# Ending a layer in PSUM: identity products for the residual, sums and squares on ScalarE, a written order, and two changes beside it

## The chip, the cores and the metric

The kernel runs on one core of one Trainium2 chip. The metric is the device time of one execution in microseconds (us), measured without the profiler as a median of several runs; the trace comes from one more execution, taken under the profiler. Engines are named as the profile names them: PE is TensorE's matmul, PEld its weight load, DVE is VectorE, ACT is ScalarE, POOL is GpSimd, and SP is SyncE, which here only issues transfers.

## The reference, cut to what matters

A two-layer encoder over 512 tokens of width 1024. Each layer is a mixer (attention in layer 0, a gated linear recurrence in layer 1) and then a mixture of 16 experts. Each sublayer ends in a residual sum and a layer norm:

```
h = layer_norm(ALPHA * h + mixed, *norm1[layer])
h = layer_norm(ALPHA * h + grouped_moe(h, router_w, router_bias, *experts[layer]), *norm2[layer])
```

The router gives each token two experts with gates that sum to one. An expert computes `silu(t @ w1) * (t @ w3)`, then `@ w2`, and its rows are scaled by the gates and summed. `layer_norm` subtracts the mean, divides by the root of the variance plus 1e-5, and applies a gain `g` and a bias `b`.

## The kernel before, in words

All matrix work is done in fp32r pairs: a weight or an activation is split into a rounded high part H (a cast on ACT, L131 for weights) and a low part L (a subtraction on DVE, L132), and a product takes three matmuls. Weights come as 1 MB chunks in order of use over the SP queue into rings of buffers; `Stream.conv_to(n)` converts parts up to the n-th. The order of instructions on each engine is set when the program is built, by a scheduler that takes what it holds to be ready, earlier lines first. Inside `tc.manual_schedule` the named engines keep the order in which the code is written; `issue_after(x)` puts an engine's instructions behind x on that engine.

**From the router to expert 0.** `route_tail` ends the first layer norm tile by tile (four tiles of 128 tokens), stores the normalized rows to `hbuf` in HBM, and computes for each token its two experts as one-hot rows `oh`, and its places in their lists (`route_p` on PE, `route_v` on DVE). At most CAP = 96 tokens of an expert are handled at once. Two small products per tile give `idx`, the list of tokens of each expert (L478, L480). `moe` then gathers expert 0's 96 rows from `hbuf` by an indirect transfer on POOL (`gather`, L552), transposes them on PE (`x_t`, L565), splits them into H and L (L566, L567), and starts the first products (`w13`, L583 to L588).

**An expert.** `w13` is 48 matmuls of 512 columns, `glu` an activation (L594) and a multiplication (L595), `h_t` four transposes (L603) and a split (L604, L605), and `w2` 24 matmuls (L629 to L631) into two PSUM banks `py`. `scatter` scales `py` by the gate on ACT (L639, two halves) and adds the 96 rows to `ybuf` in HBM by an indirect accumulating transfer on POOL (L640). To hide `glu` and `h_t`, `jobs` sets expert e's `w13` ahead of expert e-1's `w2`; only the last expert is different: the order there is `w13(14) w2(13) w2(14) w13(15) w2(15)`.

**The end of a layer.** When all scatters have landed, four accumulating transfers on POOL add `ybuf` to the residual rows `hs[t]` in SBUF (L780; ALPHA has been multiplied in before). Expert 15 is not scattered: `direct` multiplies a one-hot matrix `ot` with its scaled rows on PE (L664, L665, two halves per tile, `pd`). `tail` then does the second layer norm by a string TAIL of steps: `a` (or `p` and `q` for the halves) adds `pd` to `hs[t]` on DVE and sums the rows (L801), `m` computes the mean and the squares (L325 on DVE, L330 on ACT), `v` or `g` subtracts the mean and multiplies the gain (L809, L834, DVE), `e` or `v` takes the root (L335 on DVE, L336 on POOL), `h` multiplies it and adds the bias (L813, DVE), `k` does the same on ACT and POOL (L818, L819), and `f` hands the tile on. In layer 0 `f` is `feat_tile`: transposes on PE (L1054) and the split of the next mixer's input (L1057 on ACT, L1058 on DVE), and the mixer's first products (L1072 to L1074) take tiles 0 and 1 first. In layer 1 `f` stores the tile to `out` (L1732). Layer 0's tail is in written order on ACT and DVE, layer 1's is not.

PSUM has eight banks: tag `h` four, tags `t` and `r` two each.

Of the kernel before, what the change touches and what calls it, by code (L numbers as in the profile page):

```python
# [19 lines left out]
P = 128  # L20
D = 1024
# [9 lines left out]
TAIL = ("p0 q0 m0 p1 q1 m1 e0 p2 g0 e1 h0 q2 m2 g1 f0 h1 p3 q3 m3 e2 f1 g2 c4 h2 e3 f2 g3 h3 f3",  # L31
        "a0 m0 a1 m1 v0 a2 m2 v1 k0 f0 a3 m3 v2 h1 f1 v3 h2 f2 h3 f3")
# [163 lines left out]
class K:  # L196
# [143 lines left out]
    def route_begin(self, l):  # L340
        self.l = l
        rp = self.rp
# [48 lines left out]
    def logits_b(self, t, q, hT):  # L391
        nc = self.nc
        pl = self.ps.tile([P, 512], F32, name=f"pl{self.l}_{t}{q}", tag="t")
        for j in range(4):
            nc.tensor.matmul(pl[:, :E], hT[:, j], self.grw[:, 4 * q + j], start=j == 0, stop=j == 3)
# [67 lines left out]
    def route_v(self, a, z):  # L463
# [7 lines left out]
        V.tensor_reduce(pos, tr, axis=AX.X, op=ALU.add)  # L471
        for t in range(a, z):
# [84 lines left out]
    def x_t(self, xg, nm):  # L557
# [3 lines left out]
        for q in range(2):  # L561
            pt = self.ps.tile([P, 4, CAP], F32, name=f"xt{nm}{q}", tag="t")
            for j in range(4):
# [44 lines left out]
    def w2(self, st, key, H, L, nm, la, last=False):  # L608
# [3 lines left out]
        for fc in range(FC):  # L612
# [19 lines left out]
            mm = []  # L632
        return py
# [10 lines left out]
    def direct(self, py, gate, src, nm):  # L644
# [64 lines left out]
    def moe(self, l, st, hs, after, on_done):  # L709
        nc, tc = self.nc, self.tc  # L710
        self.hs = hs
        self.s2 = [self.rp.tile([P, 2], F32, name=f"s2{l}{t}", tag="s1", bufs=4) for t in range(NT)]
        st.limit = st.where["moe_end", l]
        xg, X, HT, gi = {}, {}, {}, []
        seq = [e for e in range(OV + 1)] + ["o"] + [e for e in range(OV + 1, E)]

        def gather(i):
# [4 lines left out]
            gi.append(self.last_gather)  # L722
# [1034 lines left out]
```

## Time and profile before

| what | value |
|---|---|
| time, median of 3 runs (lowest, highest) | 1131.86 us (1131.6, 1134.7) |
| time of the profiled execution | 1139.46 us |
| its span, first to last instruction | 1137.5 us |
| PE busy | 1044.2 us, 92% of the span |
| DVE busy | 906.9 us, 80% |
| ACT busy | 766.1 us, 67% |
| POOL busy | 240.8 us, 21% |
| mean granted clock of TensorE | 0.957 of full speed |

The profiled execution is 7.6 us longer than the median, so stretches are read from it and differences are carried over to the median. A busy share is a mean over stages with different limits; what a change is worth is read in its own stage, from what each engine waited for there. Times in the trace are counted from the first instruction.

### The profile page before, as it was taken

To read this page: it belongs to the slowest core of one execution; us is meant where nothing else is said; L and a number is where in the kernel's file an instruction comes from. 1 tells how busy PE (TensorE), PEld (TensorE's weight loads), DVE (VectorE), ACT (ScalarE), POOL (GpSimd) and SP (SyncE) were. 2 spreads that over 40 slices of the span, in tenths; PEclk is the share of its full clock that TensorE was granted. 3 is DMA by queue.
4 is the path that set the end of the run, shared out by engine and by line. 5 is a ranking of instruction groups with operands and counts; after the bars stand their busy time and mean duration, and the time that the engine had idled before them with its cause. 6 is when DMAs were issued, how large, how long until landed. Compare 5 with 4: busy or idle time off the path is not lost. (4 is left out here: it accounts for less than half of the span.)

```text
span 1137.5 us, 14945 instructions
## 1 busy us (share of the span) xinstructions
PE 1044.2 (92%) x5010; PEld 765.1 (67%) x5010; DVE 906.9 (80%) x1481; ACT 766.1 (67%) x1112; POOL 240.8 (21%) x238
## 2 busy tenths in 40 slices
PE   7999898995999999999979999995999999998992
PEld 5677677883677777776558657774677777775651
DVE  5586778558999999997886597848999999996775
ACT  5456688333878888786744899233878888786762
POOL 1113555315123111120210000014123111120132
PEclk9898999996999999999979999996999999999996
DMA  8181010696999999989953203496999999997983
GB/s 298 56 259 38 1 38 1 229 344 208 358 327 365 361 357 359 357 306 361 311 127 120 70 14 111 155 380 206 359 316 375 362 358 365 365 335 248 332 254 101
DMA packets 132980, 281.22 MB, mean 247 GB/s; under 512 B 8905, under 2 KB 32617, under 8 KB 132769
## 3 DMA queue, kind: packets, MB, share of 16 engines
q1 hardware_dynamic: 121344, 245.20, 60.0%
q0 software_dynamic: 10928, 33.93, 12.3%
q10 hardware_dynamic: 624, 1.08, 0.3%
q8 instruction: 41, 0.67, 0.2%
q14 instruction: 43, 0.34, 0.1%
HBM read 261.41 MB, written 23.74 MB: 251 GB/s over the span
## 5 line engine op out<-in xcount | busy, mean ns | idle before, releaser
L132 DVE TENSOR_TENSOR wl<-rr,wh 128x1024 fp32r<-128x1024 f32 x180 | 212.1, 1219 | 17.3 <-ACT wh L131 16.3
L131 ACT CAST wh<-rr 128x1024 fp32r<-128x1024 f32 x180 | 180.2, 1049 | 40.2 <-PE p L587 33.0
L132 DVE TENSOR_TENSOR wl<-rf,wh 128x1024 fp32r<-128x1024 f32 x104 | 124.0, 1220 | 20.8 <-ACT wh L131 20.3
L131 ACT CAST wh<-rf 128x1024 fp32r<-128x1024 f32 x104 | 105.2, 1048 | 46.6 <-DMA rf<-l_w_out 26.0
L132 DVE TENSOR_TENSOR wl<-raw,wh 128x1024 fp32r<-128x1024 f32 (+1 forms) x101 | 119.1, 1207 | 16.9 <-ACT wh L131 16.9
L131 ACT CAST wh<-raw 128x1024 fp32r<-128x1024 f32 (+1 forms) x101 | 100.9, 1033 | 30.5 <-PE ppx L1073 8.1
L583 PE MATMUL p<-wh,xh 128*96 128x512 f32 x256 | 103.3, 404 | 1.5 <-ACT xh L566 1.5
L629 PE MATMUL py<-wh,hh 128*96 128x512 f32 x256 | 101.4, 404 | 3.0 <-ACT y L639 1.9
L630 PE MATMUL py<-wl,hh 128*96 128x512 f32 x256 | 101.5, 396 | 1.6 <-DVE wl L132 1.6
L631 PE MATMUL py<-wh,hl 128*96 128x512 f32 x256 | 101.1, 398 | 0.9 <-DVE hl L605 0.9
L585 PE MATMUL p<-wh,xh 128*96 128x512 f32 x256 | 101.2, 395 | 0.3
L587 PE MATMUL p<-wh,xl 128*96 128x512 f32 x256 | 101.4, 396 | 0.0
L584 PE MATMUL p<-wl,xh 128*96 128x512 f32 x256 | 101.3, 396 | 0.0
L586 PE MATMUL p<-wl,xh 128*96 128x512 f32 x256 | 101.0, 395 | 0.0
L588 PE MATMUL p<-wh,xl 128*96 128x512 f32 x256 | 101.0, 395 | 0.0
L640 POOL DMA_INDIRECT ybuf<-y,dst x30 | 58.9, 1964 | 178.5 <-ACT y L639 151.8
L552 POOL DMA_INDIRECT xg<-hbuf,idx x32 | 35.4, 1108 | 237.3 <-PE xt L565 199.6
L132 DVE TENSOR_TENSOR wl<-rx,wh 128x1024 fp32r<-128x1024 f32 x56 | 66.3, 1219 | 8.4 <-ACT wh L131 8.4
L131 ACT CAST wh<-rx 128x1024 fp32r<-128x1024 f32 x56 | 56.2, 1050 | 9.8 <-PE p L587 9.1
L629 PEld LDWEIGHTS py<-wh,hh 128*96 128x96 f32 x256 | 41.4, 163 | 19.8 <-ACT y L639 3.4
L631 PEld LDWEIGHTS py<-wh,hl 128*96 128x96 f32 x256 | 41.7, 163 | 19.2 <-DVE hl L605 1.8
L585 PEld LDWEIGHTS p<-wh,xh 128*96 128x96 f32 x256 | 41.5, 162 | 19.3 <-ACT wh L131 1.2
(426 smaller groups left out, 2438.9 us busy)
## 6 DMA issues: line engine op xcount, KB each, us to landing
rr<-l_w SPq DMA_DIRECT2D x124, 512.0 KB, 11.3
rf<-l_w SPq DMA_DIRECT2D x68, 512.0 KB, 13.1
rr<-l_w SPq DMA_DIRECT2D x28, 1024.0 KB, 14.2
rx<-l_w SPq DMA_DIRECT2D x36, 512.0 KB, 12.0
raw<-l_w SPq DMA_DIRECT2D x36, 512.0 KB, 13.2
rf<-l_w SPq DMA_DIRECT2D x15, 1024.0 KB, 12.6
raw<-l_w SPq DMA_DIRECT2D x13, 1024.0 KB, 8.5
raw<-l_w_in SPq DMA_DIRECT2D x11, 1024.0 KB, 5.6
```

The source lines that it names most:

```text
L131: nc.scalar.copy(h[:, :w], r[:, a:a + w])
L132: nc.vector.tensor_tensor(l[:, :w], r[:, a:a + w], h[:, :w].bitcast(F32), op=ALU.subtract)
L583: nc.tensor.matmul(p1, H[:, kc], w1h[:, sl], start=f, stop=False)
L584: nc.tensor.matmul(p1, H[:, kc], w1l[:, sl], start=False, stop=False)
L585: nc.tensor.matmul(p3, H[:, kc], w3h[:, sl], start=f, stop=False)
L586: nc.tensor.matmul(p3, H[:, kc], w3l[:, sl], start=False, stop=False)
L587: nc.tensor.matmul(p1, L[:, kc], w1h[:, sl], start=False, stop=e)
L588: self.last_mm = nc.tensor.matmul(p3, L[:, kc], w3h[:, sl], start=False, stop=e).ins
L629: nc.tensor.matmul(py[n], H[:, c], a, start=c == 0, stop=False)
L630: nc.tensor.matmul(py[n], H[:, c], b, start=False, stop=False)
L631: nc.tensor.matmul(py[n], L[:, c], a, start=False, stop=c == FC - 1)
L640: nc.gpsimd.indirect_dma_start(out=self.ybuf[l], out_offset=bass.IndirectOffsetOnAxis(ap=dst, axis=0), in_=y, in_offset=None, bounds_check ...
```

## The change

Three things are done at once.

1. **Expert 0's rows come from a product.** `route_v` makes for each tile a selection matrix `sel` (128 tokens by 96 places) from the place that each token has in expert 0's list. `first_x` multiplies the normalized tiles with it in fp32 on PE, 8 products for each tile into two banks of tag `h`; the result is expert 0's input, already transposed. The first pair of tiles is done behind the last router product, the second pair at the end of `route_tail`. `x_t` takes these banks; the gather of expert 0 and its transposes are gone, and the gathers of experts 1 and 2 are issued at once.
2. **The last experts' order.** It becomes `w13(14) w2(13) w13(15) w2(14) w2(15)`, with expert 15's `h_t` in the middle of `w2(14)`. Expert 14's scatter is then issued after `w2(14)`, which is right ahead of `w2(15)`.
3. **The tail.** `pre` multiplies the identity matrix with `hs[t]` in fp32 into the `pd` banks (two products of 512 columns per tile), and `post` accumulates expert 15's rows onto it. `s` sums the rows from PSUM on ACT (two halves), `m` computes the mean on DVE and squares the halves from PSUM on ACT, `v` subtracts the mean and multiplies the gain from PSUM on DVE into `hs[t]`, `e` adds the two sums of squares and takes the root, `h` as before. Both layers' tails are in written order on ACT and DVE. Layer 1's last tile is finished and stored in halves (`z`).

```diff
-TAIL = ("p0 q0 m0 p1 q1 m1 e0 p2 g0 e1 h0 q2 m2 g1 f0 h1 p3 q3 m3 e2 f1 g2 c4 h2 e3 f2 g3 h3 f3",
-        "a0 m0 a1 m1 v0 a2 m2 v1 k0 f0 a3 m3 v2 h1 f1 v3 h2 f2 h3 f3")
+TAIL = ("s0 m0 v0 s1 e0 m1 v1 h0 e1 s2 h1 f0 m2 v2 e2 s3 f1 h2 m3 v3 e3 f2 c4 h3 f3",
+        "s0 m0 v0 s1 e0 m1 v1 h0 f0 e1 s2 h1 f1 m2 v2 e2 s3 h2 f2 m3 v3 e3 z3")
...
         V.tensor_reduce(pos, tr, axis=AX.X, op=ALU.add)
+        p0 = wp.tile([P, n], F32, name=f"p0{l}{a}", tag=f"p0{a}", bufs=1)
+        V.tensor_tensor(p0, tr[:, 0, :, 0], tr[:, 1, :, 0], op=ALU.add)
+        for t in range(a, z):
+            self.sel[t] = wp.tile([P, CAP], F32, name=f"sel{l}{t}", tag="sel", bufs=NT)
+            V.tensor_scalar(self.sel[t], self.iota16[:, :CAP], p0[:, t - a:t - a + 1], None, op0=ALU.is_equal)
...
+    def first_x(self, u, a, z):
+        if a == 0:
+            self.x0 = [self.ps.tile([P, 512], F32, name=f"x0{self.l}{q}", tag="h", bufs=4)[:, :4 * CAP]
+                       .rearrange("p (j c) -> p j c", j=4) for q in range(2)]
+        for t in range(a, z):
+            for kc in range(KC):
+                self.nc.tensor.matmul(self.x0[kc // 4][:, kc % 4], u[t][:, kc * P:(kc + 1) * P], self.sel[t],
+                                      start=t == 0 and kc % 4 == 0, stop=t == NT - 1 and kc % 4 == 3)
...
                 nc.tensor.matmul(py[n], L[:, c], a, start=False, stop=c == FC - 1)
             mm = []
+            if fc == 1 and mid:
+                mid()
...
-        def mm(t):
+        def pre(t):
             r = []
             for n in range(2):
+                r.append(self.ps.tile([P, 512], F32, name=f"pd{nm}{t}{n}", tag="h", bufs=4))
+                nc.tensor.matmul(r[n], self.ident, self.hs[t][:, n * 512:(n + 1) * 512], start=True, stop=False)
+            return r
+
+        def post(t, r):
+            for n in range(2):
                 sl = slice(n * 512, (n + 1) * 512)
-                ps = self.ps.tile([P, 512], F32, name=f"pd{nm}{t}{n}", tag="h", bufs=4)
-                nc.tensor.matmul(ps, oh[:, t], yH[:, sl], start=True, stop=False)
-                nc.tensor.matmul(ps, oh[:, t], yL[:, sl], start=False, stop=True)
-                r.append(ps)
-            return r
-        return mm
+                nc.tensor.matmul(r[n], oh[:, t], yH[:, sl], start=False, stop=False)
+                nc.tensor.matmul(r[n], oh[:, t], yL[:, sl], start=False, stop=True)
+        return pre, post
...
-            r += [(e, "a"), (e - 1, "b")] if e < E - 1 else [(e - 1, "b"), (e, "a")]
+            r += [(e, "a"), (e - 1, "b")]
...
-        gather(0)
-        port = self.rp.tile([P, 1], F32, name=f"port{l}", tag="port")
-        with tc.issue_after(gi[0]):
-            nc.gpsimd.memset(port, 0.0)
-            gather(1)
-        X[0] = self.x_t(xg[0], f"{l}_0")
-        gather(NXG)
+
         first = st.where["moe", l]
+        gather(1)
+        gather(2)
         with tc.issue_after(self.last.ins), tc.issue_after(self.last_sig):
-            free = nc.vector.tensor_copy(self.rp.tile([P, 1], F32, name=f"free{l}", tag="port"), port).ins
-            with tc.issue_after(free):
-                st.conv_to(first + 6)
+            st.conv_to(first + 2)
+            X[0] = self.x_t(None, f"{l}_0", self.x0)
+            st.conv_to(first + 6)
...
-            py = self.w2(st, (l, e), *HT[e], nm, LA, e == E - 1)
+            def mid():
+                if e == E - 2:
+                    HT[E - 1] = self.h_t(hm, f"{l}_{E - 1}", "x")
+
+            py = self.w2(st, (l, e), *HT[e], nm, LA, e == E - 1, mid)
...
+        def s(t):
+            for n, sl in enumerate(halves):
+                nc.scalar.activation(junk[:, sl], psd[t][n], AF.Identity, accum_out=self.s2[t][:, n:n + 1])
 
         def m(t):
             st[t] = self.ln_mu(self.s2[t], f"{l}2{t}")
-            self.ln_sq(st[t], hs[t], f"{l}2{t}", "vl", self.hl2)
+            for n, sl in enumerate(halves):
+                nc.scalar.activation(junk[:, sl], psd[t][n], AF.Square, bias=st[t][0], accum_out=sq[t][:, n:n + 1])
 
         def v(t):
-            mu, ss, ve, rs = st[t]
-            V.scalar_tensor_tensor(hs[t], hs[t], mu, g, op0=ALU.add, op1=ALU.mult)
+            for n, sl in enumerate(halves):
+                V.scalar_tensor_tensor(hs[t][:, sl], psd[t][n], st[t][0], g[:, sl], op0=ALU.add, op1=ALU.mult)
+
+        def e(t):
+            V.tensor_scalar(st[t][1], sq[t][:, 0:1], sq[t][:, 1:2], None, op0=ALU.add)
             self.ln_rs(st[t])
...
+        for t in (0, 1):
+            psd[t] = pre(t)
         for t in range(NT):
-            psd[t] = mm(t)
+            if t > 1:
+                psd[t] = pre(t)
+            post(t, psd[t])
...
+        with self.tc.issue_after(self.last_pl):
+            self.first_x(u, *pairs[0])
         self.sigmoid(*pairs[1])
...
         self.route_v(*pairs[1])
+        self.first_x(u, *pairs[1])
```

## Rows read from the trace of the kernel before

**Rows 1.** Windows: stretch, length, busy PE, PEld, DVE, ACT, POOL, clock, DMA, GB/s.
```profile
300.00:545.00 245.00, 243.74 (x1190) 173.84 (x1189) 221.77 (x279) 195.82 (x243) 45.06 (x30) 1.00 1.02 350
```

**Rows 2.** Timeline of PE, layer 0, from the router to expert 0.
```profile
269.40 0.17 PE L461 MATMUL pp<-ohs,half 128*128 128x16 f16 x1 [4.85 <-DVE ohs L452]
...
277.43 1.51 PE L565 MATMUL xt<-call,xg 96*128 96x96 f32 x8 [6.02 <-DMA xg<-hbuf,idx]
278.91 0.74 PE L583 MATMUL p<-wh,xh 128*96 128x512 f32 x1
...
282.01 0.41 PE L584 MATMUL p<-wl,xh 128*96 128x512 f32 x1
```

**Rows 3.** Timeline of PE, layer 1, the same place.
```profile
781.84 0.17 PE L461 MATMUL pp<-ohs,half 128*128 128x16 f16 x1 [4.91 <-DVE ohs L452]
...
794.10 0.39 PE L584 MATMUL p<-wl,xh 128*96 128x512 f32 x1
```

**Rows 4.** Windows, layer 0, expert 0's first products.
```profile
279.00:282.00 3.00, 3.00 (x7) 1.97 (x8) 2.96 (x4) 0.46 (x1) 3.00 (x4) 0.50 0.83 312
```

**Rows 5.** Instructions on tile `ot`, durations in ns (min/median/max).
```profile
L652 DVE TENSOR_SCALAR ot<-half,row x8: 275/276/391, 553.0 to 1092.0; 96x128 fp32r<-96x128 f16 x8
```

**Rows 6.** Timeline of PE: fp32 products and transposes at either clock.
```profile
257.20 1.00 PE L395 MATMUL pl<-grw,hT 128*128 128x16 f32 x8
...
586.04 1.94 PE L1054 MATMUL ftm<-call,xr 128*128 128x128 f32 x8 [3.23 <-DVE xr L813]
...
621.58 3.60 PE L1123 MATMUL pg<-xc,gw 128*128 128x512 f32 x8
```

**Rows 7.** Timeline of PE, layer 0, the last experts.
```profile
545.38 0.39 PE L630 MATMUL py<-wl,hh 128*96 128x512 f32 x1
545.61 0.39 PE L631 MATMUL py<-wh,hl 128*96 128x512 f32 x1
546.92 0.47 PE L629 MATMUL py<-wh,hh 128*96 128x512 f32 x1 [0.93 <-ACT y L639]
...
572.06 0.39 PE L631 MATMUL py<-wh,hl 128*96 128x512 f32 x1
```

**Rows 8.** Timeline of PE, layer 1, last products of experts 13 and 15.
```profile
1082.64 0.39 PE L631 MATMUL py<-wh,hl 128*96 128x512 f32 x1
...
1110.66 0.39 PE L631 MATMUL py<-wh,hl 128*96 128x512 f32 x1
```

**Rows 9.** Timeline of ACT, layer 1, expert 13's output.
```profile
1083.22 1.26 ACT L639 ACTIVATE y<-py,gpos 96x512 f32<-96x512 f32 x2
```

**Rows 10.** Timeline of POOL, both layers: scatter of expert 14, accumulations.
```profile
556.74 2.36 POOL L640 DMA_INDIRECT ybuf<-y,dst  x1 [3.04 <-ACT wh L131]
566.14 3.62 POOL L780 DMA_DIRECT2D xr<-ybuf  x4 [7.03 <-DMA ybuf<-y,dst]
...
1093.69 2.48 POOL L640 DMA_INDIRECT ybuf<-y,dst  x1 [2.90 <-ACT wh L131]
1100.44 3.62 POOL L780 DMA_DIRECT2D xr<-ybuf  x4 [4.27 <-DMA ybuf<-y,dst]
```

**Rows 11.** Tile `xr`, 555 to 610 us: the four accumulations' transfers.
```profile
DMA to landing us min/median/max: 5.4/8.4/11.9
```

**Rows 12.** The page's transfers: issues, size, median us from issue to landing.
```profile
hbuf<-xr POOLq DMA_DIRECT2D x6, 512.0 KB, 3.3
```

**Rows 13.** Timeline, layer 0: DVE's first residual sum, the next mixer's first products.
```profile
574.45 0.69 DVE L801 SCALAR_TENSOR_TENSOR xr<-xr,pd 128x512 f32<-128x512 f32 x1 [0.50 <-PE pd L665]
...
589.20 0.80 PE L1072 MATMUL ppx<-x,wh 128*128 128x256 f32 x2 [1.22 <-ACT x L1057]
```

**Rows 14.** Timeline, layer 1: DVE's first residual sum, its last step, POOL's last root.
```profile
1111.77 0.69 DVE L801 SCALAR_TENSOR_TENSOR xr<-xr,pd 128x512 f32<-128x512 f32 x1 [0.59 <-PE pd L665]
...
1129.18 1.28 DVE L813 SCALAR_TENSOR_TENSOR xr<-xr,lw,b 128x1024 f32<-128x1024 f32 x1 [0.66 <-POOL lw L336]
...
1128.59 0.55 POOL L336 TENSOR_TENSOR lw<-lw,mhalf 128x1 f32<-128x1 f32 x1 [2.66 <-DVE lw L335]
```

More of the change, by code (lines that the diff above doesn't have):

```diff
@@ L341, in route_begin @@
         self.l = l
+        self.sel = {}
         rp = self.rp
@@ L394, in logits_b @@
         for j in range(4):
-            nc.tensor.matmul(pl[:, :E], hT[:, j], self.grw[:, 4 * q + j], start=j == 0, stop=j == 3)
+            self.last_pl = nc.tensor.matmul(pl[:, :E], hT[:, j], self.grw[:, 4 * q + j], start=j == 0, stop=j == 3).ins
         x = self.lg[:, t]
@@ L561, in x_t @@
         for q in range(2):
-            pt = self.ps.tile([P, 4, CAP], F32, name=f"xt{nm}{q}", tag="t")
-            for j in range(4):
+            pt = pts[q] if pts else self.ps.tile([P, 4, CAP], F32, name=f"xt{nm}{q}", tag="t")
+            for j in range(4 if pts is None else 0):
                 kc = 4 * q + j
@@ L606, in h_t, with w2 @@
         return H, L
-    def w2(self, st, key, H, L, nm, la, last=False):
+    def w2(self, st, key, H, L, nm, la, last=False, mid=None):
         nc = self.nc
@@ L711, in moe @@
         self.hs = hs
-        self.s2 = [self.rp.tile([P, 2], F32, name=f"s2{l}{t}", tag="s1", bufs=4) for t in range(NT)]
+        self.s2 = [self.rp.tile([P, 4], F32, name=f"s2{l}{t}", tag="s1", bufs=4) for t in range(NT)]
         st.limit = st.where["moe_end", l]
-        xg, X, HT, gi = {}, {}, {}, []
+        xg, X, HT, gi = {}, {}, {}, {}
         seq = [e for e in range(OV + 1)] + ["o"] + [e for e in range(OV + 1, E)]
@@ L783, in moe @@
         st.limit = len(st.parts)
+        conv = None
         if l == 0:
             st.conv_to(done + 2)
-            with tc.manual_schedule(engines={mybir.EngineType.Activation, mybir.EngineType.DVE}):
-                self.tail(l, py, gate, self.idx[:, E - 1:E], g, b, on_done, lambda n: st.conv_to(done + n))
-        else:
-            self.tail(l, py, gate, self.idx[:, E - 1:E], g, b, on_done)
+            conv = lambda n: st.conv_to(done + n)
+        with tc.manual_schedule(engines={mybir.EngineType.Activation, mybir.EngineType.DVE}):
+            self.tail(l, py, gate, self.idx[:, E - 1:E], g, b, on_done, conv)
     def tail(self, l, py, gate, src, g, b, on_done, conv=None):
@@ L795, in tail @@
         psd, st = {}, {}
-        mm = self.direct(py, gate, src, f"{l}_{E - 1}")
-        def a(t, ns=(0, 1)):
-            for n in ns:
-                u = hs[t][:, n * 512:(n + 1) * 512]
-                V.scalar_tensor_tensor(u, u, 1.0, psd[t][n], op0=ALU.mult, op1=ALU.add, accum_out=self.s2[t][:, n:n + 1])
+        pre, post = self.direct(py, gate, src, f"{l}_{E - 1}")
+        halves = [slice(n * 512, (n + 1) * 512) for n in range(2)]
+        full = slice(0, D)
+        junk = self.hl2.tile([P, D], BF16, name=f"tj{l}", tag="vl", bufs=HX)
@@ L815, in k, with h @@
-        def k(t):
-            for n in range(2):
-                sl = slice(n * 512, (n + 1) * 512)
-                nc.scalar.mul(hs[t][:, sl], hs[t][:, sl], st[t][3])
-                nc.gpsimd.tensor_tensor(hs[t][:, sl], hs[t][:, sl], b[:, sl], op=ALU.add)
+        def h(t, sl=full):
+            V.scalar_tensor_tensor(hs[t][:, sl], hs[t][:, sl], st[t][3], b[:, sl], op0=ALU.mult, op1=ALU.add)
         def f(t):
             on_done(t, hs[t])
-        def p(t):
-            a(t, (0,))
-        def q(t):
-            a(t, (1,))
@@ L830, in e, with z @@
-        def e(t):
-            self.ln_rs(st[t])
-        def gain(t):
-            V.scalar_tensor_tensor(hs[t], hs[t], st[t][0], g, op0=ALU.add, op1=ALU.mult)
+        def z(t):
+            for sl in halves:
+                h(t, sl)
+                on_done(t, hs[t], sl)
+        for t in (0, 1):
+            psd[t] = pre(t)
         for t in range(NT):
-            psd[t] = mm(t)
-        fn = dict(a=a, m=m, v=v, h=h, k=k, f=f, p=p, q=q, e=e, g=gain, c=conv)
+            if t > 1:
+                psd[t] = pre(t)
+            post(t, psd[t])
@@ L839, in tail @@
+        fn = dict(s=s, m=m, v=v, h=h, f=f, e=e, z=z, c=conv)
         for x in TAIL[l].split():
@@ L961, in out_proj @@
                 for t in range(NT):
-                    s1.append(self.rp.tile([P, 2], F32, name=f"s1{nm}{t}", tag="s1", bufs=4))
+                    s1.append(self.rp.tile([P, 4], F32, name=f"s1{nm}{t}", tag="s1", bufs=4))
                     for kc in range(KC - 2, KC):
@@ L1731, in build @@
         k.wp = wp = L("moe1")
-        k.moe(1, st, hs, lambda: None, lambda t, u: nc.sync.dma_start(out[0, t * P:(t + 1) * P], u))
+        k.moe(1, st, hs, lambda: None,
+              lambda t, u, sl=slice(0, D): nc.sync.dma_start(out[0, t * P:(t + 1) * P, sl], u[:, sl]))
         wp.release()
```

9 lines of the change are left out of this document (4 added, 5 removed).

## The prediction

> **What bounds the kernel now.** I read the page first, then the windows of the expert stages, then engine by engine the three places that the change touches. In the windows view PE is busy for 243.7 of 245 us between 300 and 545 us, at full clock, and DVE for 221.8 [rows 1]: the experts are bound by PE, so time that is won or lost ahead of them or behind them goes one to one into the total. Two kinds of place are left where PE waits.
>
> The first is the way from router to expert 0. The timeline of PE shows it waiting for the one-hot rows until 269.40, then for the gather until 277.43, and starting expert 0 at 278.91, at half clock [rows 2, 4]. From the one-hot rows to the eighth product of expert 0 it is 282.01 - 269.40 = 12.6 us in layer 0 and 794.10 - 781.84 = 12.3 us in layer 1 [rows 2, 3].
>
> The second is the end of a layer. DVE takes up the first residual sum at 574.45, released by PE, and the next mixer's first products start at 589.20, released by the second tile's split [rows 13]; the products run on without a gap from there. In layer 1 DVE starts at 1111.77 and begins the last step at 1129.18, for 1.28 us, so it ends at 1130.46 [rows 14]. What the reader must see beside this is the chain on POOL: expert 14's scatter goes out at 556.74, the accumulations behind it at 566.14 [rows 10], and the first of them lands no sooner than 5.4 us later [rows 11], at 571.5, or 2.9 us before DVE asks for it. This is all the slack that the chain has.
>
> **Part 1, expert 0's input by a product.** Behind the one-hot rows DVE does five short instructions (the two for the places, `p0`, two selections); none should be dearer than the 0.28 us of the nearest form [rows 5], so at most 1.4, and I take 1.2. Then come 16 fp32 products of 96 columns. The nearest rows are eight in 1.00 us at full clock and eight transposes in 1.94 us at half clock [rows 6], so 2.0 to 3.9; PE has been idle and I take 3.8, with 0.2 for the small index products among them. The first half's H copy runs under the last of them. Expert 0's eighth product starts seven steps behind its first: at full clock a step is 545.61 - 545.38 = 0.23 us [rows 7], so 1.6; before, at half clock, the seven took 282.01 - 278.91 = 3.1 [rows 2, 4]. As PE has by then run some 4 us without a pause, as it had before it regained full clock in [rows 2], I take full clock and 1.7. The first pair of tiles adds three more DVE instructions ahead of the last tile's residual, which DVE has no room for: 0.55. Its 16 products lie in the time in which PE waits for the one-hot rows (4.85 us [rows 2]); without this cover they would cost 2.0 to 3.9. For the conversions that must now come faster I set 0.3. Sum: 1.2 + 3.8 + 0.2 + 1.7 + 0.55 + 0.3 = 7.75. The gain is 12.6 - 7.75 = 4.85 and 12.3 - 7.75 = 4.5, together 9.35. Bounds: all at full clock 3.8 more; expert 0 at half clock and the conversions a part late, 2.3 less in each layer, so 4.7 to 13.1. The gathers of experts 1 and 2 are issued at once on POOL; expert 1's rows have the whole of expert 0's 48 products (11 us) to land, so they cost nothing; the last tile's store to HBM comes off the path too.
>
> **Part 2, the last experts' order.** Work on PE from the end of expert 13's `w2` is 48 + 24 + 24 products either way. Before, it waits there for the bank `py` (545.61 + 0.23 = 545.84 to 546.92, 1.1 us) and again for `glu` and the split of expert 15, and ends at 572.3 [rows 7]. After, it is 72 products (16.6) and four transposes (0.45) to the end of `w2(14)`, 1.1 for `py`, 24 products (5.5): 545.84 + 23.7 = 569.5, which is 2.8 earlier. In layer 1 the same sum gives 1082.87 + 23.7 = 1106.5 against 1110.9 [rows 8].
>
> But the scatter of expert 14 now stands at the end of `w2(14)`. In layer 0 that is 545.84 + 17.05 = 562.9. ACT's scaling of both halves ended 1.6 us after PE at the same step of expert 13 (1082.87 to 1083.22 + 1.26 [rows 8, 9]), and 0.25 goes by to the issue: 564.7, against 556.74 before, 8.0 later. In layer 1: 1099.9, 1101.8, against 1093.69, 8.1 later. From scatter to accumulations it took 9.4 us in layer 0, under the weight loads, and 6.75 in layer 1, when these were over [rows 10]; they are over at 564.7 too, so I take 6.75 for both (bounds 6.75 and 9.4). The accumulations go out at 571.5 and 1108.5. The first lands 5.4 later; with issues 3.6 us in all and 11.9 at most to land [rows 10, 11] the four come some 2.6 apart: tile 0 at 576.9 and 1113.9, tile 1 at 579.5 and 1116.5. Expert 15's rows are ready some 2.1 us behind PE's end (572.3 to 574.45 [rows 7, 13]), at 571.6 and 1108.6. So it is the residual that now comes last, by 5.3 us, and PE's 2.8 and 4.4 us buy nothing.
>
> A rule speaks for more here: the Trainium skill, "DMA: Bandwidth & Descriptors", section "Anatomy of one DMA — SWDGE (gpsimd) path", puts such a transfer at about 2.0 us and its bytes at 436 GB/s, which for 512 KB would be an estimate of 3.2 us. A plain store of this size from POOL's queue shows 3.3 [rows 12], so it agrees there; the accumulations show 5.4 at the least [rows 11], and by the rule the residual would be 2.2 us earlier.
>
> **Part 3, the tail.** The identity products want the residual, and in the order of the code both tiles' products stand ahead of expert 15's rows for tile 0: PE waits for tile 1's residual. An fp32 product of 512 columns takes 3.60 / 8 = 0.45 at full clock, nearer 0.43 from start to start [rows 6], and PE, idle for 7 us by then, will be at half: 0.86, two per tile. Then two products for the first half. So sums start 1.7 + 0.9 + 0.1 behind tile 1's residual: 582.2 and 1119.2. Were tile 0's products put through first, it would be 2.6 sooner.
>
> From there ACT and DVE are worked out in the written order. A half on ACT from PSUM is 0.63 [rows 9], with reading the sum an estimated 0.66; a whole row step on DVE is 1.28, a half 0.69, about 0.1 less from start to start, and POOL's root is 0.55 [rows 14]. Counted from the first sum: `s0 m0 s1 m1` with two means 6.0; DVE's `h0` ends at 7.1; `e1` and its root 8.0; `h1` 9.2. Layer 0: `f0`'s subtractions 10.4, `mu2` 10.6, `m2` on ACT 12.0, `s3` 13.3, `f1`'s first cast 13.9; I take 14.1 for the PE transposes at half clock between `post` products (up to 16 if tile 3's come first). The mixer starts at 582.2 + 14.1 = 596.3 against 589.20: 7.1 later. Tiles 2 and 3 have the 13 us of the first half's products to follow and cost nothing. Layer 1: `mu2` 9.3, `m2` 10.7, `s3` 12.0, `h2` 12.9, `mu3` 13.1, `m3` 14.4, root 15.4, the two halves of `z3` 16.7: 1135.9 against 1130.46, 5.4 later, less an estimated 0.5 for a last transfer of half the size: 4.9. Without the late residual the tail itself is quicker: 14.1 against 14.75 in layer 0 and 16.7 against 18.7 in layer 1 from the first sum. The loads of `g` and `b` are taken to go out ahead of the scatter, as their buffers come free during `w13(15)`.
>
> **Sum.** 7.1 + 4.9 - 9.35 = +2.65 us on the profiled 1139.46, or on the median of 1131.86: 1134.5. A measurement of this kernel can tell about 0.3% (3.4 us) from no change, so this is within it.
>
> **The rivals.**
> Tile 0 first (23%): PE takes `post` of tile 0 before it waits for tile 1. For it: the scheduler takes what it holds to be ready; against: the code's order. 2.6 less in layer 0, 2.1 in layer 1, some of it lost to the second tile: 1130.6.
> The residual in time (5%): the tails start behind PE at 571.6 and 1108.6. -3.5 and -5.7 with the start's 9.35: 1113. Against it stand all of rows 10 and 11.
> Accumulations as quick as a plain store (7%), 3.3 and half the spacing [rows 12]: tile 1 is 3.4 sooner in both layers, 1127.7. The skill's rule is this case; none of the accumulations seen did it.
> Slower, identity products ahead of the last `w2` (5%): if PE's queue has them amid `w2(15)`, its second half (12 products, 5.2 at half clock) and the 2.1 behind it follow tile 1's residual: 7.3 per layer, 1149. It decides when any product of expert 15 starts behind an identity product.
> Slower, `g` and `b` beside the scatter (10%): if they stand behind it on POOL, 1 MB more at the stage's 350 GB/s [rows 1] is some 3 us ahead of the accumulations of each layer: 1140.5.
> Slower, the start gives half (10%): conversions starve expert 0, or its clock stays low, 2.3 per layer: 1139.
>
> **Numbers.** The forecast case has 40%, its own range 1132 to 1138. Faster by over 0.3% (below 1128.5): the two quick cases (12%), a third of tile 0 first (8%) and the low tail of the forecast (2%), 22%. Slower (above 1135.3): the three slow cases but for a few chances that stay below (22%), and four tenths of the forecast, as 1134.5 lies close to that bound (16%), 38%. The rest, 40%, is within. The range 1127 to 1142 leaves out the residual in time and the identity products ahead, and tails of some 7%.
>
> **What would show it.** Right: expert 0's eighth product some 8 us behind the one-hot rows; no gather for it; the accumulations issued some 2 us behind PE's last product of expert 15, where they stood 6 us ahead of it in layer 0; PE idle behind `w2(15)` and released by a transfer; the first identity product near 577 less the start's gain. Wrong: DVE or ACT in the tail released by PE with the residual long there; PE's last `w2` broken by identity products; expert 0 waiting for `wl`.

## The result, and the profile after

The changed kernel took 1150.87 us (median of 4 runs, 1145.04 to 1155.67) beside 1131.73 for the kernel before: ratio 1.0143, 95% interval 1.0099 to 1.0188, so some 16 us slower. (The two medians lie 19.1 apart; in the later comparisons the kernel before took 1135 to 1137 us, and ratios are turned into us with 1135.) The forecast was 1134.5, with a range of 1127 to 1142: a miss, on the slow side.

The profiled execution took 1150.01 us with a span of 1148.2, which is 10.7 more than the span of before. The runs say 16 (11 to 21); the profiled execution of before was 7.6 us above its own runs, and what is left between the two numbers has not been traced. Stretches are compared in the traces, kernels by their ratios.

**The start of the experts.** Timeline of PE in the changed kernel, layer 0; these lines answer to [rows 2].

```profile
267.51 0.17 PE L462 MATMUL pp<-ohs,half 128*128 128x16 f16 x1
...
268.73 0.91 PE L495 MATMUL x<-sel,xr 128*128 128x96 f32 x6 [0.95 <-DVE sel L477]
...
270.42 2.45 PE L495 MATMUL x<-sel,xr 128*128 128x96 f32 x20
272.66 0.45 PE L598 MATMUL p<-wh,xh 128*96 128x512 f32 x1
...
274.43 0.39 PE L599 MATMUL p<-wl,xh 128*96 128x512 f32 x1
```

Nothing stands between the one-hot rows (267.51) and expert 0's eighth product (274.43) but 0.95 us of waiting for the selections, 3.9 us of selection products and seven steps: 6.92 us, where it was 12.61. In layer 1 it is 795.28 - 788.37 = 6.91.

**The end of a layer.** Timeline of POOL, both layers, for [rows 10]:

```profile
558.71 1.54 POOL L657 DMA_INDIRECT ybuf<-y,dst  x1 [13.05 <-ACT y L656]
564.97 3.62 POOL L799 DMA_DIRECT2D xr<-ybuf  x4 [4.72 <-DMA ybuf<-y,dst]
...
1104.42 1.56 POOL L657 DMA_INDIRECT ybuf<-y,dst  x1 [13.06 <-ACT y L656]
1110.48 3.62 POOL L799 DMA_DIRECT2D xr<-ybuf  x4 [4.50 <-DMA ybuf<-y,dst]
```

Tile `xr` from 555 to 610 us, the accumulations' transfers of layer 0, for [rows 11]:

```profile
DMA to landing us min/median/max: 8.1/10.9/13.8
```

Timeline of PE: the last product of the last `w2`, the identity products (L680) and the mixer's first product, for [rows 7, 8, 13]:

```profile
563.31 0.40 PE L646 MATMUL py<-wh,hl 128*96 128x512 f32 x1
...
573.10 5.45 PE L680 MATMUL pd<-xr,call 128*128 128x512 f32 x8 [9.39 <-DMA xr<-ybuf]
...
582.21 2.56 PE L680 MATMUL pd<-xr,call 128*128 128x512 f32 x4 [1.84 <-DVE xr L833]
...
595.12 0.80 PE L1093 MATMUL ppx<-x,wh 128*128 128x256 f32 x2 [2.63 <-ACT x L1078]
...
1109.03 0.40 PE L646 MATMUL py<-wh,hl 128*96 128x512 f32 x1
...
1116.08 5.32 PE L680 MATMUL pd<-xr,call 128*128 128x512 f32 x8 [6.65 <-DMA xr<-ybuf]
```

PE has done its last expert and then waits 9.39 and 6.65 us, released by the accumulations: the residual is what comes last, as forecast. Windows of layer 0's end: stretch, length, busy PE, PEld, DVE, ACT, POOL, granted clock, DMA, GB/s:

```profile
536.00:564.00 28.00, 26.35 (x112) 16.87 (x110) 24.41 (x30) 20.80 (x26) 4.17 (x4) 1.00 0.82 274
564.00:579.00 15.00, 5.90 (x11) 2.81 (x12) 1.34 (x3) 0.43 (x1) 3.62 (x4) 0.66 0.93 201
```

In the 15 us before the first sum ACT and DVE are all but idle, and the clock falls from full to a mean of 0.66. The tail of layer 1, ACT's sums (L824) and squares (L829) with what they waited for, and DVE's last step; these answer to [rows 14]:

```profile
1121.89 0.60 ACT L824 ACTIVATE tj<-pd 128x512 bf16<-128x512 f32 x1 [11.74 <-PE pd L687]
...
1128.71 0.60 ACT L824 ACTIVATE tj<-pd 128x512 bf16<-128x512 f32 x1 [0.93 <-PE pd L687]
...
1132.17 0.69 ACT L829 ACTIVATE tj<-pd,lw 128x512 bf16<-128x512 f32 x1 [1.92 <-DVE lw L325]
...
1136.82 0.69 ACT L829 ACTIVATE tj<-pd,lw 128x512 bf16<-128x512 f32 x1 [2.04 <-DVE lw L325]
```

```profile
1140.02 1.42 DVE L840 SCALAR_TENSOR_TENSOR xr<-xr,lw,b 128x512 f32<-128x512 f32 x2 [0.66 <-POOL lw L336]
```

The last step ends at 1141.44. One row can be used for every kernel: from the one-hot rows to expert 0's eighth product (start), from there to the first sum of the tail on DVE or ACT (experts), and from there to the mixer's first product in layer 0 or the end of DVE's last step in layer 1 (tail). All are differences of such lines, in us; the prediction's numbers are set beside them. The start begins at the one-hot rows' products on PE, and what delays these is not in it (x1_start, below).

| kernel | start, 0 | experts, 0 | tail, 0 | start, 1 | experts, 1 | tail, 1 | ratio to before |
|---|---|---|---|---|---|---|---|
| before | 12.61 | 292.44 | 14.75 | 12.26 | 317.67 | 18.69 | 1 |
| as predicted | 7.75 | 300.2 | 14.1 | 7.75 | 325.1 | 16.7 | 1.002 |
| after | 6.92 | 304.61 | 16.08 | 6.91 | 326.61 | 19.55 | 1.0143 |
| x1_start | 6.91 | 292.61 | 14.75 | 6.91 | 317.65 | 18.71 | 0.9919 |
| x2_order | 12.28 | 298.30 | 16.75 | 12.42 | 319.06 | 17.61 | 1.0114 |
| x3_tail | 12.51 | 301.99 | 14.69 | 12.11 | 322.76 | 19.68 | 1.0152 |
| x13_start_tail | 6.91 | 303.40 | 17.37 | 6.91 | 323.97 | 19.69 | 1.0126 |
| x5_behind_w2 | 6.92 | 295.10 | 14.69 | 6.91 | 319.33 | 19.53 | 0.9986 |
| x6_tile0 | 6.91 | 302.60 | 14.70 | 6.91 | 324.56 | 19.56 | 1.0126 |
| x7_no_scatter14 | 6.90 | 293.17 | 14.70 | 6.92 | 318.62 | 19.53 | 0.9987 |
| x9_means_first | 11.35 | 304.75 | 15.75 | 11.29 | 326.22 | 18.33 | 1.0168 |
| x10_load_behind | 6.92 | 301.57 | 16.09 | 6.91 | 326.52 | 19.55 | 1.0096 |
| x11_double | 6.91 | 297.95 | 17.89 | 6.91 | 323.35 | 19.93 | 1.0103 |
| x12_free_order | 6.91 | 295.68 | 16.08 | 6.91 | 320.06 | 18.04 | 0.9993 |
| x13_no_cover | 13.22 | 293.89 | 14.76 | 13.56 | 315.94 | 18.70 | 1.0039 |

The first row against the third: starts -11.0, experts +21.1, tails +2.2, together +12.3; ahead of layer 0's one-hot rows the changed kernel is 1.9 sooner (269.40 to 267.51), which makes most of the difference to 10.7.

### The profile page after: what moved, and what is told of

Same layout as the page of the kernel before. It is cut to its first block, busy times and chain, and to the rows that moved or that the text cites. A ratio compares the mean times of both kernels' runs of the same rounds, so it can differ in the third digit from the quotient of the medians.

```text
span 1148.2 us, 15284 instructions
## 1 busy us (share of the span) xinstructions
PE 1069.3 (93%) x5154; PEld 784.0 (68%) x5154; DVE 900.3 (78%) x1477; ACT 776.2 (68%) x1158; POOL 257.3 (22%) x232
## 5 line engine op out<-in xcount | busy, mean ns | idle before, releaser
L603 PE MATMUL p<-wh,xl 128*96 128x512 f32 x256 | 100.9, 394 | 0.0
L567 POOL DMA_INDIRECT xg<-hbuf,idx x30 | 33.0, 1099 | 203.1 <-PE xt L580 167.3
L645 PEld LDWEIGHTS py<-wl,hh 128*96 128x96 f32 x256 | 41.3, 161 | 19.7 <-DVE wl L132 4.6
L601 PEld LDWEIGHTS p<-wl,xh 128*96 128x96 f32 x256 | 41.3, 161 | 18.5 <-DVE wl L132 0.7
## 6 DMA issues: line engine op xcount, KB each, us to landing
rr<-l_w SPq DMA_DIRECT2D x120, 512.0 KB, 11.3
raw<-l_w SPq DMA_DIRECT2D x13, 1024.0 KB, 11.3
```

The source lines that it names most:

```text
L601: nc.tensor.matmul(p3, H[:, kc], w3l[:, sl], start=False, stop=False)
L603: self.last_mm = nc.tensor.matmul(p3, L[:, kc], w3h[:, sl], start=False, stop=e).ins
L645: nc.tensor.matmul(py[n], H[:, c], b, start=False, stop=False)
```

## The experiments

**One part at a time.** The three parts of the diff alone, and the two that share no line with the order. x1_start keeps of the diff only `sel`, `first_x` and the gathers; x2_order only `jobs` and `mid`; x3_tail only TAIL, `pre`, `post` and the steps; x13_start_tail is the changed kernel with

```diff
-            r += [(e, "a"), (e - 1, "b")]
+            r += [(e, "a"), (e - 1, "b")] if e < E - 1 else [(e - 1, "b"), (e, "a")]
```

> Only the start is changed (expert 0's rows by a product); last order and tail as before. Theory: the way from the one-hot rows to expert 0's eighth product takes 6.9 us in both layers, as in the trace of the changed kernel, against 12.6 and 12.3, so 5 to 7.5 us come off each layer and the time is 9 to 13 us below the kernel before (ratio 0.989 to 0.992). Rival: the gain is given back behind it (conversions, gathers of later experts, a lower clock) and the ratio is within 0.003 of 1.

Measured 0.9919 (0.9890 to 0.9947): 9.2 us faster, and the start at 6.91 in both layers. Nothing is given back behind the start, as the experts and tail columns show. Something is given back ahead of it. Timeline of PE, layer 1:

```profile
770.90 7.05 PE L495 MATMUL x<-sel,xr 128*128 128x96 f32 x32
777.79 0.17 PE L462 MATMUL pp<-ohs,half 128*128 128x16 f16 x1
```

The first pair's selection products run here at a granted clock of 0.51, and the one-hot rows' products stand behind them: DVE had the rows ready at 775.91, PE takes them up 1.9 us later, without a wait of its own. The start column begins at that moment and does not see the delay. Counted from the one-hot products of the first pair of tiles (765.63 here, 771.91 before), expert 0's eighth product comes after 19.07 us where it took 22.19, so the gain is 3.1 us in layer 1 and by the same count 3.4 in layer 0, not 5.35 and 5.7. In the changed kernel, where the first pair ran at 0.68 and took 5.42 us, it is 4.8 and 5.0.

> Only the order of the last experts is changed. Theory (the late residual): expert 14's scatter goes out 8 us later, and the first residual sum on DVE waits for an accumulation's landing, some 6 us later than before in layer 0 (34.7 us behind the end of w2(13), as in the changed kernel) and 3 us in layer 1 (32.0): 9 us slower in all, ratio 1.006 to 1.010. Rival (the residual in time): glu and split of expert 15 are hidden, PE ends 2.8 and 4.4 us earlier and the sums start with it: ratio 0.992 to 0.996.

Measured 1.0114 (1.0086 to 1.0141). Timeline of DVE, its first residual sum in each layer:

```profile
578.21 0.69 DVE L807 SCALAR_TENSOR_TENSOR xr<-xr,pd 128x512 f32<-128x512 f32 x1 [7.55 <-DMA xr<-ybuf]
...
1119.30 0.69 DVE L807 SCALAR_TENSOR_TENSOR xr<-xr,pd 128x512 f32<-128x512 f32 x1 [4.60 <-DMA xr<-ybuf]
```

In [rows 13, 14] PE released these sums; here an accumulation does, after 7.55 and 4.60 us of waiting. The late residual is shown, somewhat dearer than expected.

> Only the tail is changed (identity products, sums and squares on ScalarE, written order); start and order of experts as before. Theory: layer 0's residual is there when PE ends, but the identity products (0.86 us each at full clock, double what was priced) and a tail of 16 us from the first sum to the mixer make that end some 4 us later; layer 1 has its residual early, its tail of 19.5 us against 18.7 makes some 1.5: 4 to 7 us slower, ratio 1.003 to 1.006. Rival A (the tail as priced in the prediction, 14.1 and 16.7 us): 0 to 3 us faster. Rival B: the identity products stand amid the last w2 and split it: 7 us slower per layer, ratio 1.012.

Measured 1.0152 (1.0123 to 1.0181): 17 us, which is rival B. Timeline of PE at layer 0's end:

```profile
571.18 2.08 PE L663 MATMUL pd<-xr,call 128*128 128x512 f32 x2 [7.06 <-DMA xr<-ybuf]
573.05 0.85 PE L603 MATMUL ht<-call,hm 96*128 96x96 f32 x4
573.69 1.97 PE L663 MATMUL pd<-xr,call 128*128 128x512 f32 x2
```

With the old order the scheduler puts identity products (L663) ahead of expert 15's transposes (L603). PE waits there for the residual, and the whole last `w2` comes behind it: 9.5 us in layer 0, 5 in layer 1 (experts columns). So the ratio of this run says nothing yet of the tail itself.

> The changed kernel with the order of the last experts as before. Theory: start minus 9 to 13, tail plus 4 to 7, nothing shared between the two: 3 to 8 us faster than the kernel before (ratio 0.993 to 0.997), and so some 22 us faster than the changed kernel, in which order and tail together cost more than each alone. Rival (the tail is the cost, not the order): ratio 1.005 or more.

Measured 1.0126 (1.0082 to 1.0169), for the same reason; the wait of PE is 7.77 us. The expectation of 0.993 to 0.997 failed.

**The tail without the block.** x5_behind_w2 takes x13_start_tail and holds the identity products back:

```diff
-        for t in (0, 1):
-            psd[t] = pre(t)
+        with self.tc.issue_after(self.last_w2):
+            for t in (0, 1):
+                psd[t] = pre(t)
```

> Start and tail of the changed kernel, the last experts in the order of before, and PE puts the first two tiles' identity products behind the last product of the last w2 instead of ahead of it. Theory (the 10 and 5 us by which the end of w2(15) moved in the two kernels with that tail and the old order are PE waiting for the residual in front of expert 15's transposes): w2(15) ends as in the kernel with the start alone, the residual is there by then, four identity products (3.4 us, of which 2.1 lie beside the scaling of expert 15's rows) and the longer tail cost 3.5 to 4 us per layer: ratio 0.996 to 1.001. Rival A (the tail is a gain once PE isn't blocked): 0.992 or less. Rival B (the tail is itself the cost): 1.008 or more.

Measured 0.9986 (0.9962 to 1.0010), as the theory had it. Against x1_start, which has the same start and order, the tail costs 6.7 thousandths, some 7.6 us. The end of layer 1, here on PE, then in x1_start on PE and DVE:

```profile
1103.53 0.40 PE L646 MATMUL py<-wh,hl 128*96 128x512 f32 x1
1103.76 3.60 PE L678 MATMUL pd<-xr,call 128*128 128x512 f32 x8
1106.80 0.80 PE L684 MATMUL pd<-yh,ot 96*128 96x512 f32 x1
```

```profile
1101.26 0.39 PE L646 MATMUL py<-wh,hl 128*96 128x512 f32 x1
...
1102.35 0.69 DVE L811 SCALAR_TENSOR_TENSOR xr<-xr,pd 128x512 f32<-128x512 f32 x1 [0.59 <-PE pd L680]
```

The residual is there and the clock is full, and still four identity products (3.60 us) stand ahead of expert 15's rows. Counted from the start of the last product of `w2`, the first sum comes 4.33 us later (1107.86), where it comes 1.09 later in x1_start; in layer 0 it is 4.98 and 2.40. So the products hold the first sum back by 3.2 and 2.6 us. With the tail columns (+0.8 and -0.1) this is 6.6 us, close to what the ratio gives.

**The late residual taken away.** x7_no_scatter14 is the changed kernel, identity products behind `w2` as above, and

```diff
-        nc.gpsimd.indirect_dma_start(
+        if send:      # send = e < E - 2 at the call
+          nc.gpsimd.indirect_dma_start(
```

> The changed kernel, but expert 14's scaled rows are not added to the buffer in HBM (its contribution is left out; the scaling on ACT stays), so the accumulations wait for expert 13's scatter alone; identity products behind the last w2. Theory (the late residual is the cost): the first sum comes some 29.5 us behind the end of w2(13), where it came 40.7 and 37.8 behind it: 11 and 8 us less, ratio 0.995 to 0.999. Rival (identity products and tail are the cost, the landing lies beside them): at most 8 us less in all, ratio 1.007 or more.

Measured 0.9987 (0.9963 to 1.0011), 15.6 thousandths or 17.7 us less than the changed kernel. The first sum comes 566.51 - 537.24 = 29.3 us behind the end of `w2(13)` in layer 0 and as much in layer 1. With the late residual gone, the new order has the same ratio as the old one (x5_behind_w2, 0.9986): no gain that can be told, and the late residual is the price of the order.

**Tile 0 first.** x6_tile0 puts `post(0)` ahead of `pre(1)`:

```diff
-        for t in (0, 1):
-            psd[t] = pre(t)
         for t in range(NT):
-            if t > 1:
-                psd[t] = pre(t)
+            psd[t] = pre(t)
             post(t, psd[t])
```

> The changed kernel, with tile 0's products of expert 15 ahead of tile 1's identity products on PE. Theory: tile 0's first sum comes 2 to 2.5 us sooner after its residual lands, in both layers, and half of it or more is kept: 2 to 5 us faster than the changed kernel (ratio to the kernel before 1.010 to 1.0125). Rival: tile 1 is what the rest of the tail waits for, and nothing is kept: 1.014.

Measured 1.0126 (1.0097 to 1.0155). In the trace the first sum comes 2.0 us sooner in both layers, as expected; the ratio alone could not tell it from the changed kernel's. Layer 0's tail is 1.4 shorter too, but that is the clock: it stayed at 1.00 from 579 to 588 us here, while PE worked on tiles 2 and 3, where the changed kernel had 0.75 and 0.69 at the same place (582 to 588).

**The written order.** x9_means_first changes the strings of the changed kernel:

```diff
-TAIL = ("... v1 h0 e1 s2 h1 f0 m2 v2 e2 s3 f1 h2 ...",
-        "... v1 h0 f0 e1 s2 h1 f1 m2 v2 e2 s3 h2 f2 m3 v3 e3 z3")
+TAIL = ("... v1 h0 e1 h1 f0 f1 s2 m2 v2 e2 s3 h2 ...",
+        "... v1 h0 f0 e1 s2 m2 v2 h1 f1 e2 s3 m3 v3 h2 f2 e3 z3")
```

> The changed kernel with another written order of the tail: in layer 0 tile 1's split directly behind tile 0's, ahead of tile 2's sums; in layer 1 the means of tiles 2 and 3 ahead of the last steps of tiles 1 and 2 on DVE. Theory (the written order makes ACT wait 1.9 and 2.0 us for means in layer 1 and puts tile 1's cast behind two tiles' sums in layer 0): 2 to 3 us less in each layer, ratio to the kernel before 1.008 to 1.011. Rival: tiles 2 and 3 become late for the mixer in layer 0 and the gain is lost there: 1.012 to 1.014.

Measured 1.0168 (1.0132 to 1.0203): missed. Layer 1's tail is 1.2 us shorter (18.33). Layer 0's is 0.3 shorter than in the changed kernel, but 1 us longer than the 14.7 that the old string takes at full clock, which this execution had there; tile 1's cast came at 596.43, but the mixer's first product waited for a PSUM bank that tile 2's step on DVE held. Timeline of PE, then PE at the start of layer 0, then the window from there (columns as above):

```profile
600.68 0.58 PE L1093 MATMUL ppx<-x,wh 128*128 128x256 f32 x1 [3.69 <-DVE xr L833]
```

```profile
263.84 3.79 PE L495 MATMUL x<-sel,xr 128*128 128x96 f32 x32
268.83 0.17 PE L462 MATMUL pp<-ohs,half 128*128 128x16 f16 x1 [1.21 <-DVE ohs L453]
...
273.27 4.56 PE L495 MATMUL x<-sel,xr 128*128 128x96 f32 x20
...
280.18 0.39 PE L599 MATMUL p<-wl,xh 128*96 128x512 f32 x1
```

```profile
272.00:276.00 4.00, 4.00 (x22) 4.00 (x21) 2.52 (x4) 0.00 (x0) 1.23 (x1) 0.50 0.02 4
```

The start is the same code as in the changed kernel up to here, but this execution had half clock (0.50, the 1.2 GHz level) where the other had 1.00, and the same 20 records took 4.56 us in place of 2.45. That is 4.4 us in each layer by the start column; from the one-hot products of the first pair of tiles it is 21.6 us, where the changed kernel took 17.4 and x1_start 19.1. The six runs of this kernel lie between 1149.4 and 1162.5 us with mean granted clocks of 0.975 and 0.963 at the two ends. So the ratio of this experiment mixes the start's clock with the order, and says little of the order by itself.

**The landing in layer 0.** Beside the accumulations of the changed kernel, a 1 MB load of the mixer's weights is issued on SP's queue at 564.05, 0.9 us ahead of them; in x1_start it comes 6.6 us behind them. x10_load_behind moves it:

```diff
+                q = nc.gpsimd if c0 == D + 512 else nc.sync
-                nc.sync.dma_start(t.rearrange("p (a b) -> p a b", a=KC),
+                q.dma_start(t.rearrange("p (a b) -> p a b", a=KC),
```

> The changed kernel, but the third 1 MB chunk of layer 1's input weights is loaded from POOL's queue, behind the four accumulations of layer 0, where SP's queue issued it 0.9 us ahead of them. Theory (the accumulations of layer 0 land 8.1 us after issue in place of 5.4 because this load runs beside them): they land some 5.3 us after issue, layer 0's first sum and the mixer's first product come 2 to 3 us sooner, ratio to the kernel before 1.011 to 1.0125. Rival (the accumulations are slower for their place behind the scatter, not for the load): they still take 8 us to land, ratio 1.014.

Measured 1.0096 (1.0080 to 1.0112), and tile `xr` of layer 0 shows

```profile
DMA to landing us min/median/max: 5.4/8.3/11.3
```

The load was the cause of the 2.7 us. In the trace the first sum comes 3.0 us sooner; the ratio, just below the expected range, gives somewhat more.

**The identity product's price.** x11_double, on x5_behind_w2:

```diff
-                nc.tensor.matmul(r[n], self.ident, ..., start=True, stop=False)
+                for stop in (True, False):
+                    nc.tensor.matmul(r[n], self.ident, ..., start=True, stop=stop)
```

> The kernel with start and tail, old order and identity products behind the last w2, with each identity product done twice (the second overwrites the first). Theory (an identity product costs 0.86 us at full clock, double the price in the prediction, and stands on the path): the first sum comes 3.4 us later in each layer, tiles 2 and 3 some more: 7 to 11 us slower than without doubling, ratio to the kernel before 1.005 to 1.008. Rival A (0.43 us each): half of that, 1.002. Rival B (the products lie beside ACT's and DVE's work): no change, 0.9986.

Measured 1.0103 (1.0085 to 1.0122): 13 us over x5_behind_w2, more than any of the three. Timeline of PE in layer 0:

```profile
569.55 7.03 PE L679 MATMUL pd<-xr,call 128*128 128x512 f32 x16
```

Eight products are 16 records and 7.03 us: 0.88 us each, not 0.43. In the trace the experts and tails grow by 10.5 us; the products are on the path.

**Layer 1's tail in the scheduler's order.** x12_free_order leaves `manual_schedule` to layer 0 alone:

```diff
+        if l == 1:
+            self.tail(l, py, gate, self.idx[:, E - 1:E], g, b, on_done, conv)
+        else:
...
```

> The same kernel without doubling, and layer 1's tail not in written order but in the scheduler's, which has the means of tiles 2 and 3 ahead of the last steps of tiles 1 and 2 on DVE. Theory (the written order makes ACT wait 1.6 and 2.0 us for those means): layer 1's tail from the first sum to the end of the last step goes from 19.5 us to 17 to 18, ratio 0.9965 to 0.9975. Rival (the chain of the banks, PE's identity products for tiles 2 and 3, sets it): 19 us or more, no change in the ratio, 0.9986.

Measured 0.9993 (0.9974 to 1.0013), no change that can be told from x5_behind_w2, and above the expected 0.9965 to 0.9975. Layer 1's tail did go to 18.04 us, with 0.97 us of waiting for the last mean where it was 2.04; in this execution layer 0's tail took 1.4 more, with `pre(2)` at 2.56 us as in the changed kernel, against 1.98 in x5_behind_w2: the clock was 0.61 from 580 to 583 us, and 1.00 at this place in x5_behind_w2. The written order's price of 1.5 us is read from the trace alone.

**The cover of the first pair.** x13_no_cover, on x1_start, with the call also moved behind `route_v` of the second pair:

```diff
-        with self.tc.issue_after(self.last_pl):
+        with self.tc.issue_after(self.last_pp):
             self.first_x(u, *pairs[0])
```

> The kernel with the start alone, but the first two tiles' 16 selection products stand behind the last one-hot rows' products on PE, out of the time in which PE waits for those rows. Theory (16 such products cost 3.8 us at full clock and 7 at half, and 1.1 of it still lies beside DVE's selections): expert 0's eighth product comes 2.7 to 6 us later in each layer, ratio to the kernel before 0.997 to 1.002. Rival (the price in the prediction, 2.0 to 3.9 less the 1.1): 1 to 3 us per layer, ratio 0.994 to 0.997.

Measured 1.0039 (1.0018 to 1.0059), above the expected range, 12 thousandths or 13.6 us over x1_start. The start column grows by 6.3 and 6.65 us; but the one-hot rows come 1.9 us sooner without the first pair ahead of them, and from the one-hot products of the first pair of tiles the eighth product comes 4.4 and 4.8 us later than in x1_start. Timeline of PE, layer 0:

```profile
269.76 0.17 PE L462 MATMUL pp<-ohs,half 128*128 128x16 f16 x1 [4.74 <-DVE ohs L453]
...
272.94 8.59 PE L495 MATMUL x<-sel,xr 128*128 128x96 f32 x52
```

From 268 to 276 us the granted clock is 0.50 here. Taken out of the wait for the one-hot rows, the first pair's products turn the start from a gain into a loss.

## Why the prediction missed

In ratios times 1135 us, the start is worth -9.2 (x1_start), the tail +7.6 on top of it (x5_behind_w2), the order +17.8 on top of both (the changed kernel), each to some 3 to 6 us. The prediction's terms were -9.35, -3.15 (14.1 for 14.75, 16.7 for 18.7, and 0.5 for the last store) and +15.2 (first sums at 582.2 for 574.45 and 1119.2 for 1111.77). So the start was right, the order near, and the tail had the wrong sign; by this count it is 10.8 of the 13.5 us.

The split depends on the order in which the parts are put in. In the changed kernel's own trace, where everything waits for the residual, two terms of the sum are late: the first sums come 40.7 and 37.8 us behind the end of `w2(13)` where the prediction has 36.4 and 36.3, 5.8 us in all, and the tails from there take 16.08 and 19.55 us where it has 14.1 and 16.7, 4.8 us. That the tail costs, and does not gain, is shown either way; which of the two weighs more is not.

The signs that the prediction named for being right were all there: no gather for expert 0, the accumulations 1.4 us behind PE's last product of expert 15, PE idle and released by a transfer. None of them tests the price of the tail.

**Part 1: right in sum, by errors that cancel.** The second pair's selection products were priced as 16 records, at half clock, because PE had been idle: 3.8. They are 32 records and ran at full clock: 3.9. The same misreading hides in the cover: the first pair's products take 3.79 us at full clock and up to 7.05 at half, not 2.0 to 3.9, and at half they do not fit into the 4.85 us of waiting (x1_start). The 0.55 for DVE's lack of room is borne out: where PE waits for the one-hot rows (x9_means_first, x13_no_cover), they come 10.3 us behind the one-hot products of the first pair of tiles, 0.4 later than before (9.86 and 9.93). The 0.3 for conversions did not show. From those products to the eighth product the start gains 9.8 us in the changed kernel's trace and 6.5 in x1_start's, where 9.35 was forecast.

**The price of an fp32 product: the mis-sized term.** "3.60 / 8 = 0.45" [rows 6] divided by records, not by products. An fp32 product leaves two records. Groups of instructions by line, in the changed kernel (operation, count, busy time, mean ns):

```profile
L680 PE MATMUL pd<-xr,call 128*128 128x512 f32 x32 | 20.3, 777 | 19.7 <-DMA xr<-ybuf 16.0 <-DVE xr L833 3.6
L495 PE MATMUL x<-sel,xr 128*128 128x96 f32 x128 | 19.1, 317 | 1.9 <-DVE sel L477 1.9
```

The code makes 16 identity products (two layers, four tiles, two halves) and 64 selection products. The Trainium skill, "FP8 and Floating Point Precision", section "TensorE Precision Notes", has true FP32 as four passes through the array; the trace agrees, with 0.86 to 0.88 us for 512 columns where an fp32r step takes 0.23.

**Part 2: the mechanism right, three terms off.** The chain on POOL in the changed kernel, by the prediction's own steps from the end of `w2(13)` (538.13 + 0.23 and 1083.85 + 0.23): scatter 20.35 and 20.34 behind it (18.9 predicted; PE took 19.06 to the end of `w2(14)` in place of 17.05, with 0.9 of waiting for conversions, and ACT and the issue 1.3 in place of 1.85), accumulations 6.26 and 6.06 later (6.75), first landing 8.13 and 5.60 later (5.4), first sum 5.94 and 5.81 later (5.3). The largest miss is the 2.7 in layer 0, which x10_load_behind explains: the weight load starts with the end of the last `w2` in either order, the accumulations were moved from ahead of it to behind it, and the prediction did not look what else starts there. The last step came out near for the wrong reason too: tile 1's residual was not waited for, the dearer products filled that time.

**Part 3: the step that failed** is "Without the late residual the tail itself is quicker: 14.1 against 14.75 in layer 0 and 16.7 against 18.7 in layer 1 from the first sum". It counted from the first sum and set nothing for what stands ahead of it. With the residual in time, four identity products hold the first sum back by 2.6 us in layer 0 and 3.2 in layer 1 (x5_behind_w2 beside x1_start). In layer 1 the tail from the first sum takes 19.5 us, not 16.7: the written order puts `mu2` and `mu3` behind `h1` and `h2` on DVE, where each `h` waits for POOL's root, and ACT waits 1.92 and 2.04 us for means that need 0.2. Of the 2.8 us, x12_free_order recovers 1.5; the rest is PE's bank chain for tiles 2 and 3 (1.24 us of waiting remain) and small steps, not taken apart. Layer 0's 14.1 was near where the clock held: 14.7 in x3_tail, x5_behind_w2, x6_tile0 and x7_no_scatter14, with a granted clock of 1.00 while PE worked on tiles 2 and 3, and 16.1 to 17.4 where it fell there (0.75 and 0.69 in the changed kernel, 0.50 in x13_start_tail). In the changed kernel as in x5_behind_w2 tile 3's products stand ahead of tile 0's transposes, the case for which the prediction wrote "up to 16". The 0.5 for a last transfer of half the size came with no row; the changed kernel's page has 2.6 us to landing for 512 KB to `out` and 2.1 for 256 KB, which agrees.

**The rivals.** Tile 0 first did not happen, and is worth 2.0 us at the first sum where it is made to. Identity products ahead of the last `w2`, given 5%, is not what the changed kernel does, but is what its tail does under the old order (x3_tail): the new order keeps the trap shut at 17.8 us, the one line of x5_behind_w2 without that price. The loads of `g` and `b` went out at 544.0 and 545.1, ahead of the scatter, as the prediction took it. The rule of the Trainium skill ("DMA: Bandwidth & Descriptors", section "Anatomy of one DMA — SWDGE (gpsimd) path") with its estimate of 3.2 us met no accumulation: the soonest first landing in layer 0 was 5.1 us, in x13_start_tail and x5_behind_w2, and 5.4 behind the moved load.

The kernel to keep is x1_start: the first part alone beats both others, at 0.9919 of the time before.

## What to carry to other kernels

Before pricing an instruction from a row, count the calls in the code against the row's x: a product that leaves two records costs two. When work is moved ahead of the last writer of a result, follow that writer's transfer to its reader and list every load that now becomes free to start beside it. A stretch that is to show a gain must begin at a row that the change cannot delay: the one-hot rows here could be late themselves. A tail is counted from the last engine that was busy, not from its first instruction, and an identity product that waits for a late operand must be kept out of the queue ahead of work that does not need it.

## What the runs showed of the hardware

- The first of four accumulating transfers of 512 KB from POOL's queue landed 5.1 to 5.6 us after issue in layer 0 of nine kernels, and 7.9 to 8.2 in the four where a 1 MB load went out 0.5 to 0.9 us ahead of it (the changed kernel, x2_order, x6_tile0, x9_means_first); with that load moved behind, in x10_load_behind, it was 5.4. In x7_no_scatter14, issued at 547.5 while weights still loaded, it was 8.1 as well.
- A plain fp32 product of 512 columns took 0.86 to 0.88 us at full clock, as two records, where one fp32r product took 0.23.
- The same start took three times, counted from the one-hot products of the first pair of tiles to expert 0's eighth product, in 20 places (two layers in ten profiled executions): 17.4 us in seven, 19.1 in eleven, 21.6 in two. By the start column the first two are both 6.9 and the last 11.3. At 19.1 the first pair ran at half clock (7.05 us at a granted clock of 0.51 in layer 1 of x1_start), at 17.4 partly so (5.42 us at 0.68 in the changed kernel); both times PE had no wait behind it and the second pair ran at 1.00. At 21.6 the first pair ran at 1.00 (3.79 us in x9_means_first), PE then waited 1.21 us for the one-hot rows, and the second pair ran at 0.50. Why an execution takes the one way or the other was not tried.
